# An encoder block on one core: the RWKV recurrence is given one plain tile layout, and its stages are emitted in small steps of several units in turn

## The chip, the core and the metric

The kernel runs on one core of one Trainium2 chip. Its time is the device time in microseconds of one execution, from the runs' own clock. Three runs of the kernel before took 3280.66, 3298.37 and 3299.71 us, so the median is 3298.37 us. A separate profiled execution took 3270.93 us.

## What is computed

The input is one sequence of 2048 tokens of width 1024, in float32. It is RMS-normed and projected into two groups of columns. Group A (1792 columns) is an RWKV-7 mixer of 8 heads of width 64, group B (1536 columns) is a differential attention of 4 heads. Their outputs go through one output projection and a residual, and then through a gated feed-forward block with a causal convolution of width 3.

The mixer is the part that the change touches. Its core is a scan over the tokens, one 64x64 state per head:

```python
def step(S, inp):
    r_t, w_t, k_t, v_t, a_t, b_t = inp
    sa = jnp.einsum('bhvk,bhk->bhv', S, a_t)
    S = (S * w_t[:, :, None, :] + sa[..., None] * b_t[:, :, None, :]
         + v_t[..., None] * k_t[:, :, None, :])
    return S, jnp.einsum('bhvk,bhk->bhv', S, r_t)
...
y = _rwkv7_scan(r_h, w_h, k_h, v_h, -kk, kk * a_h)
mean = jnp.mean(y, axis=-1, keepdims=True)
...
return (y * g.astype(jnp.float32)).astype(h.dtype)
```

The attention needs the projections of all three of its inputs, and the output projection needs both groups for a block of tokens.

## The kernel before

The kernel is written with tile pools and a scheduler. The program text gives each instruction a place, `high_priority(offset)` moves its priority that many instructions forward, and the scheduler then fixes one order per engine. Each engine works its own order off in sequence, so an instruction whose input is late holds up all that stand behind it.

**Phase 1** has two kinds of work. The first is projections. For each of four blocks of 512 tokens (`tb`), `proj_rwkv` makes the 14 column blocks of group A (tile `mm`, 128x512, lines L211 to L213: every product is made of three, from a high and a low half of each operand). `shift` writes them to scratch in memory. Afterwards `token_major` makes the columns of group B for the blocks in the order 3, 0, 1, 2 (tile `mm`, 128x256, L243 to L245), and `finish_qk` normalizes, transposes and stores the queries and keys.

The second kind is the recurrence, `rwkv(u)`, for 16 units of 128 tokens. A unit has two chunks of 64 tokens, four pairs of heads (`i`), and two heads in a pair (`hd`). With all heads side by side it does this:

- First part: norms and decays (`st`, `lpw`, `lpa`, `nb`, `sb`), then the products inside a chunk (`sa`, L448, K = 64 rows), masked by DVE into three tiles (L450 to L452), and transposes `bt`.
- Inverse: a triangular matrix per head and chunk is sent through memory (`ed`, `el`) into another layout, solved by 31 pairs of small DVE instructions (L482, L483), and sent back (`wd`, `tt`). Two small products `zp` (L520, L527, 32x32) complete it.
- Chain, one chunk after the other, because the state of one is the input of the next: `gp` (L543), `up` (L551), `hu` (L559), and the output `y`, to which two products are added in turn for each head, L569 with 128 rows and L571 with 64 rows.
- Outputs: the normalization of `y`, the gate product (L586) and a store to `yd`.

`after` is called once per two projected column blocks and emits one unit's first part and inverse, and the rest of the unit before the last two (`LAG = 2`), all with a priority offset of 3000. Where a float32 product is not in the split form above, one matmul of the program is two records in the trace.

**Attention** (`heads`) may start when the last unit is done, because it takes over the recurrence's pools. Nine of its steps are placed between the projections of group B, one per column block (`HEADS1 = 9`, offset 400). One head for a block of 256 queries takes scores `sc` (L725, L726), a DVE pass with mask and maximum (L729), exponentials on ACT, transposes `at`, products `po` with the values and a transpose `ott` (L813). **Feed-forward** for the first 512 tokens starts with `mixed` and `out_proj` (tile `up`, L905 to L907), which need the eight heads of the first two query blocks; its large products are L966 to L968 and L1009 to L1011.

Of the kernel before, what the change touches and what calls it, by code (L numbers as in the profile page):

```python
# [19 lines left out]
P = 128  # L20
# [8 lines left out]
XUB = 7  # L29
SUB, LRB, PUB, UB = 3, 3, 3, 2  # L30
# [9 lines left out]
LAG = 2  # L40
# [99 lines left out]
def phase1(g, ctx):  # L140
# [38 lines left out]

    def spread(tb):  # L180

        rs = rsa[:, 4 * tb:4 * tb + 4]
        rx = dn.tile([P, 4, P], F32, name="rx", tag="x", bufs=XB)
        nc.vector.tensor_copy(rx, rs.unsqueeze(2).broadcast_to((P, 4, P)))
        ps = ps_mm.tile([P, 4, P], F32, name="tp", tag="mm")
# [46 lines left out]
    def token_major(tb, hT, gi):  # L232
# [4 lines left out]
        for jj in range(2):  # L237
            for q in range(KT // 2):
                for j2 in range(2):
# [6 lines left out]
                    if q == KT // 2 - 1:  # L246
                        yield 2 * jj + j2, ps

    def proj_qk(tb, hT, gi):
# [12 lines left out]
        return lambda: finish_qk(tb, gi, qz, rs)  # L262

    def finish_qk(tb, gi, qz, rs):
# [3 lines left out]
        for hl_ in range(2):  # L268
# [15 lines left out]

    def proj_v(tb, hT, gi):
# [5 lines left out]

    w = load_w("w_in_a", 12, 4, P, True)
# [3 lines left out]
    stats(0)  # L296
    rb = spread(0)
# [9 lines left out]
    mask = cp.tile([P, P], F32, name="mask")  # L307
    nc.sync.dma_start(out=mask, in_=a["c_mask"])
# [42 lines left out]
    for i in range(UB):  # L351
        tts.append(cp.tile([P, NCH, GP, C], F32, name=f"tt{i}"))
        nc.gpsimd.memset(tts[i], 0.0)
# [4 lines left out]
    hc = cp.tile([P, GP, C], F32, name="hc")  # L358
    nc.vector.memset(hc, 0.0)
    def rwkv(u):  # L360
# [8 lines left out]
        r = sp.tile([P, GP, SB], F32, name="zl", tag="zl", bufs=1)  # L369
# [3 lines left out]
        xm = [sp.tile([P, GP, 2, P], F32, name="xm", tag="xm", bufs=XUB) for c in range(NCH)]  # L373
        bk = [sp.tile([P, GP, P], F32, name="bk", tag="bk", bufs=XUB) for c in range(NCH)]
        rb = sp.tile([P, GP, 2, C], F32, name="rb", tag="rb", bufs=(XUB + 1) // 2)
        lr = sp.tile([P, NCH, GP, C], F32, name="lr", tag="lr", bufs=LRB)
# [3 lines left out]
        for p in range(GP):  # L380
            nc.scalar.activation(sq[:, p], k[:, p], AF.Square, scale=v("kk", p))
        st = ps_tp.tile([P, GP, 2], F32, name="st", tag="tp")
        for p in range(GP):
            nc.tensor.matmul(st[:, p, :], sq[:, p], ones2, start=True, stop=True)
        nst = 2 * GP
# [4 lines left out]

        lpw = ps_tp.tile([P, GP, SB], F32, name="lpw", tag="tp")
        for p in range(GP):
            nc.tensor.matmul(lpw[:, p], wda[0:64, p * P:(p + 1) * P], zw[0:64], start=True, stop=True)
        thw = sp.tile([P, GP, SB], F32, name="thw", tag="thw")
        for p in range(GP):
            nc.scalar.activation(thw[:, p], lpw[:, p], AF.Tanh, bias=hw0[:, p:p + 1], scale=0.5)
        lpa = ps_tp.tile([P, GP, SB], F32, name="lpa", tag="tp")
        for p in range(GP):
            nc.tensor.matmul(lpa[:, p], wda[64:128, p * P:(p + 1) * P], zw[64:128], start=True, stop=True)
        kh = sp.tile([P, GP, SB], F32, name="kh", tag="kh")  # L400
        for p in range(GP):
            nc.scalar.activation(kh[:, p], lpa[:, p], AF.Tanh, bias=hw0[:, 4 + p:5 + p], scale=0.5)
# [18 lines left out]
        for c in range(NCH):  # L421
            cs, kc, uc = slice(c * C, c * C + C), slice(c * C, c * C + C), slice(C - c * C, 2 * C - c * C)
            for hd in range(2):
                q = hb[hd]
                nc.vector.tensor_mul(xm[c][q, :, hd, 0:C], kkn[q, :, cs], pp[q, :, c, 0:C])
                if hd == 0:
                    nc.vector.tensor_mul(bk[c][:, :, uc], kkn[:, :, cs], an[:, :, cs])
                nc.vector.tensor_mul(xm[c][q, :, hd, C:2 * C], r[q, :, cs], pp[q, :, c, 1:C + 1])
            nc.vector.tensor_mul(bk[c][:, :, kc], kh[:, :, cs], pin[:, :, cs])
# [4 lines left out]
        nc.gpsimd.tensor_mul(rkh, kh, r)  # L434
        sb = ps_tp.tile([P, GP, 2], F32, name="sb", tag="tp")
# [5 lines left out]
        def mk(q, a, b):  # L441
            return mask[q, a:b].unsqueeze(1).broadcast_to((64, GP, b - a))
# [11 lines left out]
        bkt = bk  # L454
        for c in range(NCH):
            ps = ps_sc.tile([P, GP, P], F32, name="bt", tag="sa")
            bs = bk[c]
# [680 lines left out]
```

## Time and profile before

| | value |
|---|---|
| median of three runs | 3298.37 us |
| profiled execution | 3270.93 us, its span 3269.2 us |
| TensorE (PE) busy | 3136.8 us, 96% of the span |
| VectorE (DVE) busy | 2085.0 us, 64% |
| ScalarE (ACT) busy | 1524.9 us, 47% |
| GpSimd (POOL) busy | 661.0 us, 20% |
| mean granted clock of PE | 0.972 |

Busy time of PE counts each matmul from its start to the end of its result, and matmuls overlap in the pipeline. A busy PE is therefore not one that issues as fast as it can: how fast it issues is read from the distance between the starts of neighbouring rows.

### The profile page before, as it was taken

How to read it: one execution, taken by the hardware profiler on the slowest of the kernel's cores; microseconds unless marked ns; L12 is line 12 of the kernel's file. 1: busy time of each engine (PE TensorE's matmuls, PEld its weight loads, DVE VectorE, ACT ScalarE, POOL GpSimd, SP SyncE). 2: the span in 40 equal slices, each digit the busy share in tenths (PEclk: the TensorE clock that was granted, in tenths of full speed). 3: DMA queues.
4: the chain of work that ended last, by engine and by line, in shares of the span. 5: the costliest groups of instructions: out<-in, count | busy, mean ns of one | idle time of the engine just before them, and what ended most of it. 6: DMA issues, size and time to landing. Idle time of an engine off the chain costs nothing.

```text
span 3269.2 us, 54217 instructions
## 1 busy us (share of the span) xinstructions
PE 3136.8 (96%) x19314; PEld 2657.6 (81%) x19314; DVE 2085.0 (64%) x5939; ACT 1524.9 (47%) x3391; POOL 661.0 (20%) x501
## 2 busy tenths in 40 slices
PE   8999999999999898899999999999998999999999
PEld 6777777888888788788878888888888888888887
DVE  4788778888873565667777786666533444444444
ACT  5666555655645564444445565444423322222221
POOL 4112113342322013254444111111100000000000
PEclk9989999989999899999999999999999999999999
DMA  9765544345464977556556756565574132223222
GB/s 298 252 210 155 189 141 152 105 134 153 126 183 132 290 233 262 160 192 204 197 196 222 234 174 203 168 206 184 192 281 153 65 116 84 97 91 107 87 97 97
DMA packets 395006, 557.43 MB, mean 171 GB/s; under 512 B 82544, under 2 KB 209776, under 8 KB 394608
## 3 DMA queue, kind: packets, MB, share of 16 engines
q1 hardware_dynamic: 394736, 553.97, 52.9%
q8 instruction: 153, 2.51, 0.3%
q14 instruction: 117, 0.96, 0.1%
HBM read 440.59 MB, written 113.25 MB: 169 GB/s over the span
## 4 chain that ended last, share of the span: by engine, by line
PE 80%; DMA 9%; DVE 8%; ACT 1%; issue 1%; SPq 1%; POOL 0%; DVEq 0%; ACTq 0%; POOLq 0%
PE up L968 9%; PE up L966 9%; PE up L967 9%; PE dn L1010 5%; PE dn L1009 5%; PE dn L1011 5%; PE mm L213 3%; PE mm L211 3%; PE mm L212 3%; PE mm L243 2%; PE y L571 2%; PE y L569 2%; PE mm L244 2%; PE mm L245 2%; PE up L906 2%; DMA fwlo<-lo_w_out 2%
## 5 line engine op out<-in xcount | busy, mean ns | idle before, releaser
L967 PE MATMUL up<-hT,fwhi 128*128 128x512 f32 (+1 forms) x1536 | 581.3, 379 | 0.0
L966 PE MATMUL up<-hT,fwhi 128*128 128x512 f32 (+1 forms) x1536 | 575.4, 378 | 3.7 <-DVE halo L975 2.8
L968 PE MATMUL up<-hT,fwlo 128*128 128x512 f32 (+1 forms) x1536 | 571.6, 378 | 7.0 <-DMA fwlo<-lo_w_ffn_up 7.0
L973 DVE SCALAR_TENSOR_TENSOR yy<-up,vec,yy 128x511 f32<-128x511 f32 x352 | 262.0, 744 | 346.2 <-ACT yy L970 345.9
L1012 DVE TENSOR_TENSOR acc<-dn,acc 128x512 f32<-128x512 f32 x352 | 237.0, 688 | 184.0 <-PE dn L1011 183.2
L968 PEld LDWEIGHTS up<-hT,fwlo 128*128 128x128 f32 x1536 | 292.2, 190 | 62.6 <-DMA fwlo<-lo_w_ffn_up 10.4
L966 PEld LDWEIGHTS up<-hT,fwhi 128*128 128x128 f32 x1536 | 290.2, 190 | 57.8 <-issue 4.3
L967 PEld LDWEIGHTS up<-hT,fwhi 128*128 128x128 f32 x1536 | 291.9, 190 | 52.4
L996 POOL TENSOR_TENSOR gl<-yy,gh 128x512 fp32r<-128x512 f32 (+1 forms) x64 | 106.0, 1656 | 1006.4 <-ACT gh L995 821.8
L117 ACT CAST fwhi<-fwraw 128x1024 fp32r<-128x1024 f32 x164 | 172.5, 1052 | 266.1 <-PE up L967 185.5
L970 ACT ACTIVATE yy<-up,vec 128x512 f32<-128x512 f32 x176 | 136.6, 777 | 301.2 <-PE up L968 295.9
L1010 PE MATMUL dn<-dlo,gh 128*128 128x512 f32 x704 | 276.1, 393 | 0.9 <-DMA dlo<-lo_w_ffn_down 0.9
L729 DVE CUSTOM_DVE_ANT_0 e<-sc,nd 128x512 f32<-128x512 f32 (+3 forms) x320 | 188.3, 607 | 136.9 <-PE sc L726 112.9
L1009 PE MATMUL dn<-dhi,gh 128*128 128x512 f32 x704 | 272.5, 396 | 0.5 <-ACT gh L995 0.5
L1011 PE MATMUL dn<-dhi,gl 128*128 128x512 f32 x704 | 261.9, 393 | 0.1
L243 PE MATMUL mm<-whi,hh 128*128 128x256 f32 x768 | 232.7, 304 | 11.9 <-DVE qlo L105 5.4
L244 PE MATMUL mm<-wlo,hh 128*128 128x256 f32 x768 | 227.2, 297 | 7.7 <-DMA wlo<-lo_w_in_b 7.5
L245 PE MATMUL mm<-whi,hl 128*128 128x256 f32 x768 | 225.0, 296 | 0.0
L736 ACT ACTIVATE e<-e,nm 128x1024 f32<-128x1024 f32 (+4 forms) x192 | 171.9, 898 | 53.3 <-DVE nm L733 52.9
L211 PE MATMUL mm<-hh,whi 128*128 128x512 f32 x448 | 187.8, 421 | 9.2 <-ACT hh L201 6.9
L117 ACT CAST whi<-wraw 128x512 fp32r<-128x512 f32 x208 | 127.8, 619 | 138.5 <-PE mm L212 61.8
L213 PE MATMUL mm<-hh,wlo 128*128 128x512 f32 x448 | 187.2, 419 | 2.1 <-POOL wlo L119 2.1
(278 smaller groups left out, 7322.6 us busy)
## 6 DMA issues: line engine op xcount, KB each, us to landing
fwraw<-in_w_ffn_up_dram SPq DMA_DIRECT2D x132, 512.0 KB, 5.5
fwlo<-lo_w_ffn_up SPq DMA_DIRECT2D x88, 512.0 KB, 5.0
draw<-in_w_ffn_down_dram SPq DMA_DIRECT2D x132, 256.0 KB, 4.3
vg<-vd SPq DMA_DIRECT2D x128, 256.0 KB, 4.3
wraw<-in_w_in_a_dram SPq DMA_DIRECT2D x112, 256.0 KB, 3.5
wraw<-in_w_in_b_dram SPq DMA_DIRECT2D x96, 256.0 KB, 5.1
lo_w_ffn_up<-fwlo SPq DMA_DIRECT2D x44, 512.0 KB, 2.9
dlo<-lo_w_ffn_down SPq DMA_DIRECT2D x88, 256.0 KB, 4.9
```

The source lines that it names most:

```text
L117: nc.scalar.copy(hi, raw)
L211: nc.tensor.matmul(ps, whi[k], hh[k], start=k == 0, stop=False)
L213: nc.tensor.matmul(ps, wlo[k], hh[k], start=False, stop=k == KT - 1)
L243: nc.tensor.matmul(ps, hh[k][:, ts_], whi[k], start=k == 0, stop=False)
L244: nc.tensor.matmul(ps, hh[k][:, ts_], wlo[k], start=False, stop=False)
L245: nc.tensor.matmul(ps, hl[k][:, ts_], whi[k], start=False, stop=k == KT - 1)
L966: nc.tensor.matmul(ps[:, q], wh[:, k % 4, cs], xh, start=k == 0, stop=False)
L967: nc.tensor.matmul(ps[:, q], wh[:, k % 4, cs], xl, start=False, stop=False)
L968: nc.tensor.matmul(ps[:, q], wl[:, k % 4, cs], xh, start=False, stop=k == KT - 1)
L1009: nc.tensor.matmul(ps, gh_[:, tsl], dh_, start=gi == 0, stop=False)
L1010: nc.tensor.matmul(ps, gh_[:, tsl], dl_, start=False, stop=False)
L1011: nc.tensor.matmul(ps, gl_[:, tsl], dh_, start=False, stop=gi == FG - 1)
```

## The change

- The recurrence gets one layout. `xm`, `lr`, `rb` and `sh` go. `ar` holds both left operands and `bk` both right ones, for both chunks, and `sm` holds the whole masked product. Twelve DVE instructions that build operands become four wide ones, and twelve masking instructions per unit become four of 128x512.
- The state lives in two fixed tiles `hs`, one per chunk.
- In the chain, one product `gy` (128 rows, 128 columns) makes what `gp` and L569 made apart. Two groups of eight further products are added to it, one before `up` and one after `hu`, each group in one piece.
- Pairs of products on the lower and the upper 64 rows (`sa`, `lpw` and `lpa`), or on two groups of 32 rows (`zp`), stand next to each other in the program.
- `rwkv(u)` yields 22 times. `tick` takes one step each of the oldest unit in the chain, of one in its outputs, of one in its inverse, and one or two steps of a unit's first part; `after` makes seven ticks (`STEPS`), and at most three units are under way between first part and chain (`UNITS`).
- The transposes of `finish_qk` are put off into the next column block's products, and `spread` into the next token block's first product.

```diff
-LAG = 2
+STEPS = 7
+UNITS = 3
...
@@ token_major
                     if q == KT // 2 - 1:
                         yield 2 * jj + j2, ps
+                if 4 * jj + q in (4, 6) and fins:
+                    fins.pop(0)()
...
+    stage = {n: [] for n in ("first", "ahead", "inverse", "ready", "chain", "last")}
+    def step(n, to):
+        with tc.high_priority(offset=HP):
+            if stage[n] and next(stage[n][0], "next") == "next":
+                unit = stage[n].pop(0)
+                if to:
+                    stage[to].append(unit)
+    def tick():
+        nonlocal ticks
+        ticks += 1
+        st = stage
+        if not st["chain"] and st["ready"]:
+            st["chain"].append(st["ready"].pop(0))
+        behind = len(st["ahead"]) + len(st["inverse"]) + len(st["ready"])
+        if not st["inverse"] and not st["ready"] and (len(st["ahead"]) > 1 or st["ahead"] and not st["first"] and (not units or behind + len(st["chain"]) == UNITS)):
+            st["inverse"].append(st["ahead"].pop(0))
+        behind = len(st["ahead"]) + len(st["inverse"]) + len(st["ready"]) + len(st["chain"])
+        if not st["first"] and units and (units[0] + 1) * SB <= done * TB and behind < UNITS:
+            st["first"].append(rwkv(units.pop(0)))
+        step("chain", "last")
+        step("last", None)
+        step("inverse", "ready")
+        for _ in range(1 + (ticks % 2 or not st["chain"])):
+            step("first", "ahead")
...
@@ rwkv, first part
-            for hd, q, q_ in ((0, lo_, hi_), (1, hi_, lo_)):
-                sa = ps_sc.tile([P, GP, P], F32, name="sa", tag="sa")
-                for i in range(GP):
-                    nc.tensor.matmul(sa[:, i, :], bk[c][q, i, :], xm[c][q, i, hd, :], start=True, stop=True)
-                kb, ub = hb[c], hb[1 - c]
-                nc.vector.tensor_mul(lr[q, c], sa[ub, :, 0:C], mk(ub, 0, C))
-                nc.vector.tensor_mul(rb[ub, :, hd], sa[ub, :, C:], mk(ub, C, P))
-                nc.vector.tensor_mul(xm[c][q_, :, hd], sa[kb], mk(kb, 0, P))
+            sa = [ps_sc.tile([P, GP, P], F32, name="sa", tag="sa") for hd in range(2)]
+            for i in range(GP):
+                for hd, q in enumerate(hb):
+                    nc.tensor.matmul(sa[hd][:, i, :], bk[q, i, c], ar[q, i, c], start=True, stop=True)
+            for hd in range(2):
+                nc.vector.tensor_mul(sm[c][:, :, hd], sa[hd], mk[c])
+            yield
...
@@ rwkv, chain (before: gp, up, hu as below, one head after the other)
-            for hd in range(2):
-                for i in range(GP):
-                    nc.tensor.matmul(y4[yq, i, hd, :], xm[c][:, i, hd, C:2 * C], sh[c][:, i, hd, :],
-                                     start=True, stop=False)
-                    nc.tensor.matmul(y4[yq, i, hd, :], rb[ub, i, hd, :], su[c][ub, i, hd, :],
-                                     start=False, stop=True)
+            gy = ps_y.tile([P, GP, 2, C], F32, name="gy", tag="y")
+            for i in range(GP):
+                nc.tensor.matmul(gy[:, i], ar[:, i, c], h[:, i], start=i == 0, stop=False)
+            for n, (i, hd) in enumerate(ih):
+                nc.tensor.matmul(gy[ub, i, hd], sm[c][kb, i, hd, ub], su[c][kb, i, hd], start=False, stop=n == len(ih) - 1)
+            gt = sp.tile([P, GP, 2, C], F32, name="gt", tag="gt")
+            nc.scalar.copy(gt[ub], gy[ub])
+            yield
+            up = ps_ch.tile([P, GP, 2, C], F32, name="up", tag="ch")
+            for i, hd in ih:
+                nc.tensor.matmul(up[ub, i, hd], tt[ub, i, hd], gt[ub, i, hd], start=True, stop=True)
+            nc.scalar.copy(su[c][ub], up[ub])
+            yield
+            hu = ps_ch.tile([P, GP, C], F32, name="hu", tag="ch")
+            for i in range(GP):
+                for hd, q in enumerate(hb):
+                    nc.tensor.matmul(hu[q, i], bk[:, i, c, q], su[c][:, i, hd], start=True, stop=True)
+            for hd, q in enumerate(hb):
+                nc.vector.tensor_add(h_[q, :, hd], hu[q], hp[q])
+            for n, (i, hd) in enumerate(ih):
+                nc.tensor.matmul(gy[kb, i, hd], sm[c][:, i, hd, kb], su[c][:, i, hd], start=False, stop=n == len(ih) - 1)
+            nc.scalar.copy(yt[kb], gy[kb].rearrange("p i h d -> p (i h d)"))
+            yield "next" if c == NCH - 1 else None
...
@@ phase 1
-            after(tb)
+            after()
+        done = tb + 1
```

Three places show how the order moves on PE. The first is the end of a chunk of the chain. Before, the two products for `y` (L569 and L571) alternate, and `hu` stands among them:

```order
L571 MATMUL y<-su,rb 64x64
L569 MATMUL y<-sh,xm 64x64
L571 MATMUL y<-su,rb 64x64
L559 MATMUL hu<-su,bk 64x64 x8
L569 MATMUL y<-sh,xm 64x64
L571 MATMUL y<-su,rb 64x64
```

In the change, a chunk's products stand in blocks of one shape, here with projections (`mm`) between two of them:

```order
L577 MATMUL gy<-hs_481,ar 128x128 x4
L579 MATMUL gy<-su,sm 64x64 x8
L246 MATMUL mm<-whi,hl_13619 128x256
...
L585 MATMUL up<-gt,tt_471 64x64 x8
L278 MATMUL tp<-ident,qz 128x128 x3
...
L591 MATMUL hu<-su,bk 64x64 x8
L595 MATMUL gy<-su,sm 64x64 x8
```

The eight alternations per head half are gone from the end of the chunk.

The second place is the products `sa` of a chunk. The numbers tell the two tiles `sa` apart, which belong to the lower and the upper 64 rows. In the change they stand in turn, with another unit's or stage's instruction between some of them:

```order
L490 MATMUL sa_1254<-ar_1161,bk_1162 128x128
L490 MATMUL sa_1255<-ar_1161,bk_1162 128x128
L490 MATMUL sa_1254<-ar_1161,bk_1162 128x128
L481 MATMUL sb_1247<-rk2_446,rkh_1245 128x2 x4
L490 MATMUL sa_1255<-ar_1161,bk_1162 128x128
L490 MATMUL sa_1254<-ar_1161,bk_1162 128x128
L490 MATMUL sa_1255<-ar_1161,bk_1162 128x128
```

Before, four of one stand together, then four of the other.

The third place is between two of the first attention heads (`ott` ends one, `sc` begins a later one). Before, the projections of group B fill the room between them:

```order
L813 MATMUL ott<-ident,ot 128x128 x2
L272 MATMUL tp<-ident,qz 128x128 x4
L725 MATMUL sc<-kg,qs 128x512
L726 MATMUL sc<-kg,qs 128x512
L725 MATMUL sc<-kg,qs 128x256
L726 MATMUL sc<-kg,qs 128x256
L243 MATMUL mm<-whi,hh_14131 128x256
L244 MATMUL mm<-wlo,hh_14131 128x256
L245 MATMUL mm<-whi,hl_14139 128x256
```

In the change the heads stand almost alone:

```order
L832 MATMUL ott<-ident,ot 128x128 x2
L796 MATMUL at<-ident,e_13287 128x128
L796 MATMUL at<-ident,e_13314 128x128 x2
L820 MATMUL po<-ah,vg 128x256
L823 MATMUL po<-ah,vg 128x128
L824 MATMUL po<-al,vg 128x128
L825 MATMUL po<-ah,vg 128x128
L826 MATMUL po<-al,vg 128x256
L827 MATMUL po<-ah,vg 128x256
L924 MATMUL up<-fwhi,yT_15079 128x256
L832 MATMUL ott<-ident,ot 128x128 x2
```

Before, 864 products `mm` of 128x256 stand behind the last one for `y`, and in the change 215 stand behind the last `gy`.

## Rows read from the trace of the kernel before

**Rows 1.** The page's first part: busy time, share of the span, instructions.
```profile
PE 3136.8 (96%) x19314; PEld 2657.6 (81%) x19314; DVE 2085.0 (64%) x5939; ACT 1524.9 (47%) x3391; POOL 661.0 (20%) x501
```
**Rows 2.** Stages: length, busy time of five engines, granted clock, DMA share, GB/s.
```profile
240.00:1075.00 835.00, 808.46 (x6882) 681.93 (x6880) 640.32 (x2099) 475.54 (x1402) 227.85 (x214) 0.94 0.50 150
1075.00:1228.00 153.00, 133.14 (x937) 123.53 (x938) 94.97 (x449) 97.93 (x330) 18.18 (x13) 0.91 0.83 254
1228.00:1249.00 21.00, 13.31 (x85) 10.33 (x84) 16.58 (x49) 13.07 (x25) 1.46 (x1) 1.00 0.85 303
1249.00:1321.00 72.00, 65.84 (x501) 62.62 (x501) 38.19 (x114) 28.70 (x50) 29.57 (x14) 0.97 0.81 254
1321.00:3269.00 1948.00, 1895.28 (x9801) 1602.70 (x9800) 1130.57 (x2724) 761.15 (x1220) 327.99 (x200) 0.99 0.48 158
```
**Rows 3.** Waits of PE: total us, times, longest.
```profile
PE mm L243 <- DVE qlo L105: 5.4, 2, 4.6
PE tp L187 <- DVE rx L184: 3.2, 2, 2.5
```
**Rows 4.** Timeline of PE: blocks of one shape, and what follows each.
```profile
609.37 0.97 PE L543 MATMUL gp<-sh,xm 128*64 128x64 f32 x16
610.27 0.38 PE L437 MATMUL sb<-rk,rkh 128*128 128x2 f32 x2
...
615.45 1.05 PE L384 MATMUL st<-ones,ksq 128*128 128x2 f32 x8
616.36 0.36 PE L245 MATMUL mm<-whi,hl 128*128 128x256 f32 x1
```
**Rows 5.** Timeline of PE, outputs of a chunk: start, length, instruction.
```profile
600.20 0.33 PE L569 MATMUL y<-sh,xm 128*64 128x64 f32 x2
600.46 0.33 PE L571 MATMUL y<-su,rb 64*64 64x64 f32 x2
...
602.51 0.32 PE L571 MATMUL y<-su,rb 64*64 64x64 f32 x2
```
**Rows 6.** Timeline of PE: a change of shape from `mm` to `zp` and back.
```profile
607.55 0.28 PE L245 MATMUL mm<-whi,hl 128*128 128x256 f32 x1
607.67 0.28 PE L243 MATMUL mm<-whi,hh 128*128 128x256 f32 x1
...
607.88 0.69 PE L520 MATMUL zp<-t,lr 32*32 32x32 f32 x16
608.49 0.39 PE L243 MATMUL mm<-whi,hh 128*128 128x256 f32 x1
```
**Rows 7.** Timeline of PE: `sa` alone, and `sa` beside `lpw`.
```profile
611.88 1.16 PE L448 MATMUL sa<-xm,bk 64*128 64x128 f32 x8
612.96 0.39 PE L245 MATMUL mm<-whi,hl 128*128 128x256 f32 x1
...
621.24 0.27 PE L393 MATMUL lpw<-zw,wda 64*128 64x128 f32 x1
621.25 0.27 PE L448 MATMUL sa<-xm,bk 64*128 64x128 f32 x1
621.36 0.27 PE L393 MATMUL lpw<-zw,wda 64*128 64x128 f32 x1
621.36 0.27 PE L448 MATMUL sa<-xm,bk 64*128 64x128 f32 x1
```
**Rows 8.** Timeline of DVE: first unit's last mask, first transpose behind its solve.
```profile
128.38 0.69 DVE L452 TENSOR_TENSOR xm<-sa,mask 64x512 f32<-64x512 f32 x1
...
175.96 0.43 DVE L494 STREAM_TRANSPOSE t<-tt 32x256 f32<-32x256 f32 x1 [2.93 <-DMA tt<-wd]
```
**Rows 9.** By line: durations ns min/median/max, first and last start us.
```profile
L813 PE MATMUL ott<-ident,ot x64: 270/272/476, 1084.9 to 2355.5; 128*128 128x128 f32 x64
```
**Rows 10.** Timeline of PE: the eighth head's last product.
```profile
1213.82 0.38 PE L813 MATMUL ott<-ident,ot 128*128 128x128 f32 x2
```

More of the change, by code (lines that the diff above doesn't have):

```diff
@@ L357, in phase1 @@
         nc.gpsimd.memset(eye[q * 32:q * 32 + 32].rearrange("l j t -> l (j t)")[:, q::36], 1.0)
-    hc = cp.tile([P, GP, C], F32, name="hc")
-    nc.vector.memset(hc, 0.0)
+    hs = []
+    for c in range(NCH):
+        hs.append(cp.tile([P, GP, 2, C], F32, name=f"hs{c}"))
+        nc.vector.memset(hs[c], 0.0)
     def rwkv(u):
@@ L384, in rwkv @@
             nc.tensor.matmul(st[:, p, :], sq[:, p], ones2, start=True, stop=True)
+        yield
+        lpw = ps_tp.tile([P, GP, SB], F32, name="lpw", tag="tp")
+        lpa = ps_sc.tile([P, GP, SB], F32, name="lpa", tag="sa")
+        for p in range(GP):
+            for l, q in ((lpw, lo_), (lpa, hi_)):
+                nc.tensor.matmul(l[:, p], wda[q, p * P:(p + 1) * P], zw[q], start=True, stop=True)
+        thw = sp.tile([P, GP, SB], F32, name="thw", tag="thw")
+        kh = sp.tile([P, GP, SB], F32, name="kh", tag="kh")
+        for l, t, b in ((lpa, kh, 4), (lpw, thw, 0)):
+            for p in range(GP):
+                nc.scalar.activation(t[:, p], l[:, p], AF.Tanh, bias=hw0[:, b + p:b + p + 1], scale=0.5)
+        yield
         nst = 2 * GP
@@ L535, in rwkv @@
+        for b in range(2):
+            nc.scalar.copy(zt[r2[b]], zp[r2[b], 0])
+        yield
+        for i, hd in ih:
+            for b in range(2):
+                nc.tensor.matmul(zp[r1[b], 1, i, hd], zt[r2[b], i, hd], tt[r2[b], i, hd, 32:64], start=True, stop=True)
+        for b in range(2):
+            nc.scalar.copy(tt[r1[b], :, :, 32:64], zp[r1[b], 1])
+        yield "next"
+        w = GP * P
+        yt = sp.tile([P, w], F32, name="yt", tag="yt", bufs=2)
         for c in range(NCH):
+            kb, ub, h, h_ = hb[c], hb[1 - c], hs[c], hs[1 - c]
@@ L593, in rwkv @@
         nc.gpsimd.tensor_add(yt, yt, vt)
+        yield
+        yield
+        yield
+        y = ps_sc.tile([P, w], F32, name="y", tag="sa")
+        nc.tensor.matmul(y, zg, wgu, start=True, stop=True)
         nc.vector.tensor_mul(yt, y, yt)
         nc.sync.dma_start(out=g.yd[u * SB:(u + 1) * SB, :], in_=yt)
-    units = list(range(g.ntb * TB // SB))
-    started = []
-    def unit():
-        if units:
-            with tc.high_priority(offset=HP):
-                started.append(rwkv(units.pop(0)))
-                next(started[-1])
-        if started and (len(started) > LAG or not units):
-            with tc.high_priority(offset=HP):
-                next(started.pop(0), None)
     def head():
@@ L611, in head, with after, rest @@
             next(g.heads, None)
-    def after(done):
-        if (units and (units[0] + 1) * SB <= done * TB) or (started and not units):
-            unit()
-        if not units and not started and g.att is None and 2 in g.phases:
+    def after():
+        for _ in range(STEPS):
+            tick()
+        rest()
+    def rest():
+        if not units and not any(stage.values()) and g.att is None and 2 in g.phases:
             rctx.close()
@@ L648, in phase1 @@
                 nh += 1
-    while units or started:
-        after(nb)
+    while units or any(stage.values()):
+        tick()
+    after()
     if 2 not in g.phases:
```

194 lines of the change are left out of this document (70 added, 124 removed).

## The prediction

> **What bounds the kernel now.** I read the page's busy times first, then the table by stages, then PE's timeline inside phase 1, the waits of PE, and last the order of the changed program. PE is busy for 96% of the span [rows 1], so a gain must come from PE issuing less, issuing faster, or standing still less. The stages [rows 2] say where: the recurrence runs with the projections from about 240 to 1075 us, attention starts at 1075 while projections of group B are still being made, these end at 1228, and from 1321 on it is feed-forward with attention, 1948 us that the change does not touch. All that can change lies in the first 1321 us. There DVE is busy for 640 of 835 us in the recurrence and for 95 of 153 in the first attention stretch, so it is a second candidate, but not the one that ends most waits: PE's named waits are few [rows 3]. The recurrence therefore costs what its products cost on PE, and what counts is the distance between starts.
>
> These distances differ greatly for like work. In a block of one shape, 16 records `gp` take from 609.37 to 610.27 us, 0.056 us each, and 8 of `st` take 0.91 us, 0.114 each [rows 4]. For `y`, where records with 128 and with 64 rows alternate in twos, nine such steps go from 600.20 to 602.51 us: 0.257 for two records, 0.128 each, though they have the 64 columns of `gp` [rows 5]. A change of shape costs time at the edges of blocks too: `mm` follows `mm` after 0.12 us, but `zp` follows it after 0.21 [rows 6]. So one change of shape costs about 0.09 us. The third thing to see is two kinds of product on the two halves of the rows: 8 `sa` alone take 1.08 us (0.135 with their edges, and 0.112 by the step within a kind), but `sa` beside `lpw` start within 0.01 us of each other and the next pair comes 0.11 us later [rows 7]. Both run at once.
>
> **The change part by part**, on PE's time, against the profiled execution of 3270.93 us (27 us under the median of the runs, 3298.37).
>
> *Outputs of a chunk.* Before: 8 heads times two products times two records are 32 records at 0.128, 4.1 us, and `gp` 0.90, together 5.0. After: four products `gy` with 128 columns (8 records at 0.114, 0.91 us), eight with 64 rows (16 at 0.056, 0.90) and eight more at the end (0.90), together 2.7. Saved: 2.3 us for each of 32 chunks, **-73 us**. `up` and `hu` keep their number. Bounds: if adding to the same result is the cost and not the change of shape, 32 records keep 0.05 us each, which leaves -22; if the larger `gy` issues as fast as `gp`, -88.
>
> *Pairs of `sa`.* 256 products are 512 records at 0.112. In the new order only 105 of the 224 possible neighbours inside a chunk really stand side by side (the second place in the order shows why); each such pair hides one record: 105 x 0.112 = **-12 us**. Bounds 0 and -25. `lpw` and `lpa` stand in separate blocks of four in the new order: 0.
>
> *Pairs of `zp`.* Of 512 products 407 have a neighbour on the other group of rows. At 0.036 us per record (16 in 0.61 us, with edges [rows 6]) full overlap as in [rows 7] would give up to -15. In [rows 7] the two results were different tiles; here both go to one tile `zp`. The Trainium skill ("TensorEngine Tiling (Array Packing)", Gotcha 1: PSUM Pressure) says that different row tiles cannot access the same PSUM bank simultaneously. By that rule this term is 0, by the pairs of the trace it is -15; no row here shows such a pair on one tile. I take 0, because the step of 0.036 us is already small.
>
> *More changes of shape elsewhere.* Because steps of several units are emitted in turn, the order mixes their products more. Outside `y` I count 465 changes of shape up to the start of attention before, and 669 in all in the new order (there `gy` is included). 204 x 0.09 = **+18 us**; +10 to +30.
>
> *DVE and ACT.* Twelve operand products per unit become four, twelve masks become four. That is work off the bounding engine, so I cost it at nothing; PE covers it. It gives room to the solve, below.
>
> *Waits that go.* The transposes of the queries no longer stand right behind their own normalization (the 5.4 us of L243 behind `qlo`), nor `spread` in front of the first product (3.2 us) [rows 3]: **-7 us**, 0 to -9. Next in line there is only the next `mm`.
>
> *Where the recurrence ends.* The first part of a unit is now held back until there is room (three units), and the inverse until the next unit is ahead. In the order, 215 `mm` are left behind the last product of the chain, against 864 before; behind the first scores 77 are left, against 665. So 588 x 0.12 = 71 us of projections leave the stretch of the first heads and fill the recurrence instead. They are not lost, but the heads lose their cover. From the end of the first head to that of the eighth it took 1213.8 - 1084.9 = 129 us [rows 9, 10]. Without 71 us of projections PE would need 58. DVE's load there is 95/153 of 129, 80 us [rows 2], but this holds the splitting of queries, keys and values, which goes with the projections. Where the projections had just ended (1228 to 1249) DVE was busy for 16.6 of 21 us, 79%. At that share 50 to 80 us of DVE work take 63 to 101 us, 5 to 43 more than PE needs. I take **+15**, near the lower end because the projections' share goes.
>
> *The solve.* A unit's first `zp` waits for its way through memory, 31 steps on DVE and back. The first unit took 47.6 us from its last mask to the first transpose behind the solve (128.38 to 175.96) [rows 8]. Priced with the steps above, PE has 57 to 131 us of other work between a unit's last `sa` and its first `zp` in the old order, and 35 to 123 in the new one; the least are 35, 41 and 46. Against 47.6 this lacks 13 + 7 + 2, and the granted clock of 0.94 stretches it a little: **+8**, 0 to +22.
>
> *Clock.* The mean of 0.94 in the recurrence [rows 2] means some 12% of 835 us at 1.2 GHz. Fewer slow stretches like `y` may raise it, the heads without cover may lower it: **-8**, between -20 and +10.
>
> Sum: -73 - 12 + 0 + 18 - 7 + 15 + 8 - 8 = **-59 us**. The profiled execution becomes 3212, and the median 3239 us, 1.8% less.
>
> **The rivals.**
>
> *The heads keep their pace.* Then seven heads again take 129 us, now with only 58 us of PE work in them: +71 instead of +15, the sum is -3, and the median 3295. For it: scores, maximum, exponential, transposes and values follow one another over three engines, and DVE was busy for only 62% of the filled stretch. Against it: just behind the projections DVE was at 79% [rows 2], and there the heads' products alternated with projections by priority, so their own chain did not set the pace.
>
> *The solve ends last (slower).* If the way through the solve takes 65 us instead of 47.6, because the wide masks and the state updates of two other units stand between its 62 small instructions in DVE's order, PE stands still at `zp` in nine of the 16 units. The shortfall against the new order's room, stretched by 6% for the clock, is 130 us. The sum is -59 - 8 + 130 = +63, and the median 3361. It outweighs the gain from about 57 us on. Against it: DVE has some 16 instructions per unit less, and DVE was well occupied when the first unit took 47.6. For it: everything behind `zp` on PE, projections included, waits with it.
>
> *The alternation is not what costs.* If records that add to an earlier result are slow as such, the outputs give -22 and not -73, and the sum is -8: 3290, no change.
>
> **How the numbers follow.** The forecast gets a chance of 0.62, the heads' pace 0.17, the solve 0.14, the alternation 0.07. The predicted time is the forecast's, 3239 us. Its own bounds reach from about 3185 (full pairs and a better clock) to 3270. The range must also take in the two rivals without change, up to 3300 with the scatter of the runs, and leaves out the solve: 3185 to 3302. A difference under 1%, 33 us, can't be told from no change in this kernel. Of the forecast nine tenths lie beyond it, which with the halves of the rivals gives 0.60 for faster; no change holds the heads' pace, most of the alternation and the rest, 0.26; slower is the solve, 0.14.
>
> **What would show it.** In the changed profile `gy` with 64 columns should step at about 0.056 us per record in blocks; if it steps at 0.11 or more, the first term is wrong. `sa` records should start in twos. PE's waits should show `zp` or the products with `t11` behind DVE or the transfer of `tt` with under 25 us in all; over 60 means the solve. The first scores should start near 1075 us again, and the first large feed-forward product (1321 before) should come near 1260. If attention starts on time and that product comes after 1300, the heads kept their pace. If attention itself starts later than 1110, the recurrence is what was priced wrongly.

## The result and the profile after

The changed kernel takes 3301.14 us (median of 20 runs, 3292.53 to 3314.14), the kernel before 3277.59 us (20 runs); the ratio is 1.0065, 95% interval 1.0049 to 1.0081. Forecast were 3239 us and a gain of 59 us; the change costs 24 us. The 20 runs put the kernel before 21 us under the median of three, 3298.37, that the forecast started from. The profiled executions, before and after, have spans of 3269.2 and 3294.6 us.

The stages of the changed kernel, cut where the kernel before was cut in [rows 2]: length, busy time of five engines, granted clock, DMA share, GB/s.

```profile
240.00:1153.00 913.00, 857.58 (x7148) 749.20 (x7146) 605.99 (x2000) 520.67 (x1534) 233.77 (x214) 0.90 0.54 161
1153.00:1180.00 27.00, 21.81 (x127) 18.90 (x127) 17.67 (x98) 12.37 (x38) 1.29 (x1) 0.75 0.88 272
1180.00:1208.00 28.00, 17.46 (x88) 13.67 (x86) 18.57 (x107) 16.12 (x50) 1.27 (x1) 0.82 0.81 259
1208.00:1332.00 124.00, 106.17 (x705) 94.82 (x704) 88.03 (x332) 63.66 (x127) 40.06 (x22) 0.90 0.73 224
1332.00:3294.00 1962.00, 1899.67 (x9788) 1603.36 (x9786) 1122.11 (x2722) 758.81 (x1218) 327.91 (x200) 0.99 0.48 157
```

Attention starts at 1153 instead of 1075, and the clock in the recurrence is 0.90 instead of 0.94. The first eight heads then need little time: from the end of the first to that of the eighth it takes 1236.5 - 1166.0 = 70 us, against 129 before [rows 9, 10].

```profile
L832 PE MATMUL ott<-ident,ot x64: 270/272/476, 1166.0 to 2362.9; 128*128 128x128 f32 x64
1236.53 0.44 PE L832 MATMUL ott<-ident,ot 128*128 128x128 f32 x2
```

The first large feed-forward product comes at 1332 instead of 1321, and the untouched rest takes 1962 instead of 1948 us.

The products themselves, in PE's timeline (start, length, instruction): first `zp`, which answers to [rows 6], then the outputs of a chunk, which answer to [rows 5].

```profile
565.41 0.69 PE L557 MATMUL zp<-t,sm 32*32 32x32 f32 x32
566.04 0.39 PE L244 MATMUL mm<-whi,hh 128*128 128x256 f32 x1
...
713.98 1.05 PE L577 MATMUL gy<-hs,ar 128*128 128x128 f32 x8
714.97 1.14 PE L579 MATMUL gy<-su,sm 64*64 64x64 f32 x16
716.04 1.16 PE L435 MATMUL lpa<-zw,wda 64*128 64x128 f32 x8
...
723.78 0.69 PE L591 MATMUL hu<-su,bk 128*64 128x64 f32 x16
724.29 1.10 PE L595 MATMUL gy<-su,sm 128*64 128x64 f32 x16
725.32 0.39 PE L244 MATMUL mm<-whi,hh 128*128 128x256 f32 x1
```

The outputs of this chunk take 0.99 + 1.07 + 1.03 = 3.1 us against 5.0 before. Over all 32 chunks, by the mean distance behind their records at full clock, a chunk takes 3.43 us against 4.99. 32 records of `zp` take the 0.69 us that 16 took in [rows 6], and 16 of `hu` 0.51 us: both kinds run two at once. But elsewhere the steps of several units cut one another up. A little earlier in the same timeline:

```profile
572.36 0.37 PE L563 MATMUL zp<-tt,zt 32*32 32x32 f32 x10
572.66 0.33 PE L591 MATMUL hu<-su,bk 128*64 128x64 f32 x2
572.92 0.24 PE L563 MATMUL zp<-tt,zt 32*32 32x32 f32 x2
573.09 0.33 PE L591 MATMUL hu<-su,bk 128*64 128x64 f32 x2
...
574.02 0.33 PE L595 MATMUL gy<-su,sm 128*64 128x64 f32 x2
574.28 0.24 PE L563 MATMUL zp<-tt,zt 32*32 32x32 f32 x2
574.45 0.33 PE L595 MATMUL gy<-su,sm 128*64 128x64 f32 x2
```

Two records of each in turn, 0.43 us for four: this is the alternation that the change had taken out of `y`. And the waits of PE from 240 to 1396 us (in total, times, longest; [rows 3] of before had 5.4 behind `qlo`):

```profile
PE sc L744 <- DMA qs<-qd: 9.5, 6, 3.2
PE mm L244 <- ACT qz L258: 9.3, 7, 2.8
PE mm L244 <- DVE qlo L106: 6.5, 3, 4.3
PE mm L245 <- DMA wlo<-lo_w_in_b: 6.2, 4, 3.6
PE mm L244 <- ACT hh L202: 5.9, 6, 3.2
```

**One account for all kernels.** I took the distances between the starts of all PE records up to the 614th of the 6144 `up` records of the feed-forward (output projection included), and split what exceeds the price of each record at full clock: distances over 0.6 us are "standing", the longer price at half clock (1.2 instead of 2.4 GHz) is "clock", and the rest, less what runs at once, is "issue" (changes of shape and slow series). "Reach" is the time of that product, "rest" from there to the last PE start. The experiments e1 to e18 follow in the next section. The same program up to there differs by 7 to 10 us between two executions (before and e6, changed and e5, e1 and e7), so smaller differences say nothing. The work up to that mark is almost the same: e1 and e7 have done 57 records more there than the kernel before, e9, e10, e15 and e16 68 more, some 9 us, which their "rest" then lacks. Each row is one profiled execution; those of e3, e7, e9 and e13 lie 6 to 11 us above the median of their kernel's runs, those of e10, e15 and e17 8 to 10 below.

| kernel | reach | issue | standing | clock | rest |
|---|---|---|---|---|---|
| before / e6 | 1389 / 1399 | 163 / 163 | 88 / 88 | 65 / 75 | 1876 / 1876 |
| changed / e5 | 1396 / 1403 | 114 / 113 | 120 / 125 | 90 / 93 | 1894 / 1882 |
| y grouped, e1 / e7 | 1390 / 1400 | 99 / 98 | 121 / 130 | 91 / 92 | 1886 / 1866 |
| half solve: before e9, grouped e10, changed e8 | 1413, 1349, 1410 | 160, 101, 115 | 93, 110, 131 | 79, 58, 90 | 1861, 1863, 1869 |
| no low weights: before e13, grouped e11, changed e12 | 1406, 1331, 1405 | 164, 94, 117 | 71, 106, 132 | 92, 58, 85 | 1876, 1880, 1883 |
| pairs alone e18, with y e15, and sa e16 | 1394, 1370, 1359 | 134, 76, 70 | 101, 115, 121 | 82, 97, 88 | 1867, 1856, 1851 |

Change less kernel before: issue -49, standing +32, clock +26, rest +18. With e5 less e6 it is -50, +37, +18 and +6, so clock and rest are the uncertain two.

### The profile page after: what moved, and what is told of

The parts are those of the page before. It is cut to its first block, busy times and chain, and to the rows that moved or that the text cites. A ratio compares the mean times of both kernels' runs of the same rounds, so it can differ in the third digit from the quotient of the medians.

```text
span 3294.6 us, 53252 instructions
## 1 busy us (share of the span) xinstructions
PE 3125.0 (95%) x19058; PEld 2654.8 (81%) x19058; DVE 1994.2 (61%) x5668; ACT 1515.7 (46%) x3311; POOL 662.5 (20%) x501
## 4 chain that ended last, share of the span: by engine, by line
PE 72%; DVE 11%; DMA 10%; ACT 3%; issue 2%; SPq 2%; POOL 0%; ACTq 0%; DVEq 0%; POOLq 0%
PE up L987 9%; PE up L985 9%; PE up L986 9%; PE dn L1029 5%; PE dn L1030 4%; PE dn L1028 4%; PE mm L214 2%; PE mm L212 2%; DMA fwlo<-lo_w_ffn_up 2%; PE mm L213 2%; PE mm L244 2%; PE up L925 2%; PE mm L246 2%; PE mm L245 2%; PE up L926 2%; PE sa L490 2%
## 5 line engine op out<-in xcount | busy, mean ns | idle before, releaser
L992 DVE SCALAR_TENSOR_TENSOR yy<-up,vec,yy 128x511 f32<-128x511 f32 (+1 forms) x352 | 261.7, 743 | 378.4 <-ACT yy L989 378.3
L213 PE MATMUL mm<-hl,whi 128*128 128x512 f32 x448 | 185.3, 414 | 0.1
```

The lines of the kernel that those rows point to most:

```text
L213: nc.tensor.matmul(ps, whi[k], hl[k], start=False, stop=False)
L992: nc.vector.scalar_tensor_tensor(yn[:, d:], ps[:, 0:512 - d], w, yn[:, d:], ALU.mult, ALU.add)
```

## The experiments

**Does y's alternation cost what its steps show?** e1 is the kernel before with

```
-  for hd: for i: y <- xm, sh (start=True); y <- rb, su
+  all eight y <- xm, sh (start on the first only); then all eight y <- rb, su
```

> The kernel before with one edit: in a chunk the eight products of y with 128 rows stand together, and behind them the eight with 64 rows, instead of one of each per head. Nothing else of the change is in it. If the alternation of shapes is what costs (first term of the prediction), 32 records at 0.128 us become 32 at about 0.056 plus two changes of shape, 2.1 us less for each of 32 chunks: about -65 us, ratio 0.98, and the attention's first scores come some 65 us sooner. Rival: records that add to an earlier result are slow as such, or PE had that time to spare while it waited for the next operands: between -22 and 0 us, ratio 0.993 to 1.0.

Measured: 3284.28 us, ratio 1.0020 (1.0009 to 1.0032). The steps fell nearly as forecast: in e1's timeline 16 records take 1.1 us, and 14 of the second kind 1.0; `gp` and `y` of a chunk take 3.07 us against 4.99 in the mean. The view by line (durations, first and last start) has the first scores at 1006.8, 68 us sooner than in [rows 2].

```profile
401.27 1.15 PE L569 MATMUL y<-sh,xm 128*64 128x64 f32 x16
404.16 1.02 PE L572 MATMUL y<-su,rb 64*64 64x64 f32 x14
```
```profile
L726 PE MATMUL sc<-kg,qs x320: 220/393/793, 1006.8 to 2259.1; 128*128 128x512 f32 x136, 128*128 128x128 f32 x8, 128*128 128x256 f32 x8, 128*128 128x384 f32 x8
```

So the first term's mechanism is right, but none of it arrives. The early scores are in part a matter of order: from 240 us to them PE starts 6545 records, in [rows 2] 6882, and the other 337 follow behind. Waits of e1 from 240 to 1390 us, then two of the kernel before in the same stretch, then the stages of e1:

```profile
PE mm L244 <- DMA wlo<-lo_w_in_b: 15.2, 6, 4.2
PE sa L448 <- DVE wl L483: 13.8, 3, 5.5
PE sc L726 <- DMA qs<-qd: 10.2, 5, 3.6
```
```profile
PE mm L244 <- DMA wlo<-lo_w_in_b: 7.5, 8, 3.6
PE sc L725 <- DMA qs<-qd: 2.8, 4, 1.2
```
```profile
240.00:1007.00 767.00, 721.26 (x6545) 625.22 (x6545) 625.32 (x2056) 448.10 (x1310) 222.36 (x211) 0.91 0.51 151
1007.00:1226.00 219.00, 186.51 (x1313) 176.01 (x1314) 122.49 (x532) 128.03 (x439) 25.57 (x17) 0.89 0.78 237
```

DVE is busy for 82% of the recurrence (77% in [rows 2]), `sa` waits behind the last instruction of the solve (`wl`), weights and queries come later than before, and the clock falls from 0.94 to 0.91.

**The order of the feed-forward.** Only `HA`, which sets the heads of that stage ahead, is changed in e5 (changed kernel) and e6 (before): `-HA = 0` `+HA = 20`; e7 is e1 with `+HA = 1`.

> The changed kernel with one number changed that only acts behind the recurrence: the attention heads of the feed-forward stage are put 20 places ahead (HA 20, not 0). By the order the heads of the second feed-forward block then end behind 1200, 1322, 1483, 1624, 1771 and 1910 of its products, where the changed kernel has 1182, 1268, 1439, 1583, 1704 and 1870 and the kernel before 1190, 1346, 1486, 1622, 1769 and 1911; the order up to the first feed-forward product is that of the change. Theory that part of the loss is not in the recurrence at all but in this order, which the change moved without touching its code: the traces show 501 us for the work between the 30% and 50% marks of these products plus 70% in the kernel before and 522 in the changed one, so about -18 us, 3283. Rival: the order there is indifferent and the 20 us are scatter of one profile: 3301 plus or minus 5.

> The kernel before with the same one number (HA 20), so that its feed-forward order is the same as that of the changed kernel with HA 20 but for one head; the order of its first stage is its own. Both theories: within 5 us of the kernel before, since its order there was already the good one. Against the changed kernel with HA 20 it shows what the change is worth without the feed-forward order: by the traces up to the first tenth of the feed-forward products (1389 us before, 1396 after) the changed one is still 5 to 8 us slower; if the change's own gain was only hidden by the order, it is 20 us or more faster.

> The kernel before with y grouped, and HA 1: its feed-forward order then has the second block of the kernel before (1190, 1346, 1486, 1622, 1769, 1911), where grouped y alone had fallen into the other one (1166, 1248, 1406, 1562, 1700, 1850). Theory of the order: about -18 us against grouped y alone, 3266, ratio to before 0.997. Rival (the order is indifferent): 3284. Both say that of the 63 us of issue time that grouping takes out of the recurrence at most some 10 reach the end.

Measured: e5 3292.01, ratio 1.0031 (1.0012 to 1.0050); e6 3276.04, 1.0001 (0.9979 to 1.0022); e7 3261.11, 0.9938 (0.9918 to 0.9958). e1 and then e7 in one stretch of the feed-forward:

```profile
1900.00:2140.00 240.00, 225.67 (x1240) 191.67 (x1238) 166.41 (x473) 123.88 (x217) 26.02 (x19) 0.97 0.59 184
```
```profile
1900.00:2140.00 240.00, 230.90 (x1305) 198.12 (x1304) 171.22 (x475) 125.98 (x220) 26.96 (x21) 0.99 0.58 186
```

The same 240 us hold 1240 records in one order and 1305 in the other. One number that only acts behind the recurrence is worth 9 us to the changed kernel and 23 to e1. In these traces the order of that stage differs between kernels that differ only ahead of it, so part of a ratio here can be that order. At nearly equal order the change still costs 10 to 16 us (by the ratio, or by e5 against e6).

**Who takes the saving?** Less VectorE: `-for s in range(31)` `+for s in range(0, 31, 2)` in the changed kernel (e8), before (e9), y grouped (e10). Fewer transfers: the low weights not fetched again, in y grouped (e11), changed (e12), before (e13); both in the changed one (e17). These kernels no longer compute the function: they leave out half of the solve, or take the high half of a weight for the low one.

> The changed kernel with HA 20, and 15 of the 31 steps of each unit's solve left out: 480 instructions of 0.28 us on VectorE, some 134 us of its work (what it computes there is then not the inverse). PE's work is the same. If PE's waits and the half clock in the recurrence come from VectorE's queue and the way through the solve, the time that PE was to gain appears: about -40 us against the changed kernel with HA 20, 3252. Rival: PE's own issue and its clock bound the stretch, VectorE only follows: 0 to -10 us, 3282 to 3292.

> The kernel before with HA 20 and the same 15 steps of the solve left out. PE's named waits behind VectorE in its recurrence are some 20 us. Theory that y's slow stretches give VectorE its time: the solve is hidden there, so only -5 to -15 us, 3261 to 3271. Rival: VectorE bounds the kernel before as well, -40 us or more.

> The kernel before with y grouped, HA 20 and the same 15 steps of the solve left out (its second feed-forward block is in the order of the kernel before). Its recurrence had 82% VectorE occupation and 17 us of PE's waits of sa behind the solve's last instruction. If VectorE takes back what grouping saves, then against the kernel before with half a solve grouping now gives 45 us or more instead of 16: 3261 - 45 = 3216 or less. Rival (the clock and the attention stretch take it back): 16 to 25 us, about 3240 to 3250.

> The kernel before with y grouped and HA 1, and in all projections but the first of each weight the low halves of the weights are not fetched (the high half stands in their place, so the projections are not exact): some 35 MB of transfers less up to 1240 us, PE's products the same in number and shape. With grouped y PE waited 15 us behind these fetches and 13 us behind those of the queries, with DMA busy for 78% of the attention stretch. If transfers take back what grouping saves: -25 us against grouped y with HA 1, 3236. Rival: these waits only show who is late, and others take their place: 3261 plus or minus 8.

> The changed kernel with HA 20, and the low halves of the projections' weights are not fetched but for the first use of each weight (the high half stands in their place, so the projections are not exact). Its PE waited 11 us behind these fetches and 12 behind those of the queries even with half a solve. If transfers limit its recurrence, as they did with grouped y alone: -40 us against the changed kernel with HA 20, 3252. Rival: its limit is the order of the products of group B and of their splits on ScalarE and VectorE: 0 to -12 us, 3280 to 3292.

> The kernel before with HA 20 and the same fetches left out. If its slow y gave the transfers time, they are hidden there: -5 to -15 us against 3276, 3261 to 3271, as half a solve gave it -3. Rival: transfers end last in the attention stretch of every version: -40 us, 3236.

> The changed kernel with HA 20, with both reliefs at once: 15 of the 31 solve steps left out, and the low halves of the projections' weights not fetched but for the first use of each (the projections are not exact). Each alone gave it nothing (-8 and +2 us). If the two limits stand behind each other in the changed order: -35 us or more against 3292, 3257 or less. Rival: neither is its limit; what holds it is PE's own issue (mixed shapes, 62 us of changes behind 200 us where grouped y alone has 44) and the half clock that goes with it: 3280 to 3296.

Measured, ratio to before: e8 3283.53, 1.0009 (0.9990 to 1.0029); e9 3273.52, 0.9978 (0.9949 to 1.0006); e10 3228.26, 0.9836 (0.9800 to 0.9872); e11 3219.99, 0.9819 (0.9784 to 0.9854); e12 3294.52, 1.0059 (1.0035 to 1.0082); e13 3277.91, 1.0007 (0.9991 to 1.0024); e17 3277.20, 0.9988 (0.9963 to 1.0014). The recurrence of e10 and of e11:

```profile
240.00:978.00 738.00, 704.66 (x6542) 613.41 (x6540) 535.83 (x1630) 447.97 (x1307) 221.46 (x210) 0.94 0.53 157
```
```profile
240.00:1004.00 764.00, 722.24 (x6692) 631.66 (x6690) 624.49 (x2070) 459.29 (x1381) 226.47 (x213) 0.93 0.43 126
```

This is the clearest finding. Either relief is worth at most 4 us to the kernel before (e9, e13); with either, grouping y is worth 45 us (e10 against e9) or 58 (e11 against e13) of the 64 us of issue that it saves in the account (163 - 99), and the clock is back at 0.94 and 0.93. The order of the feed-forward is no rival for the 45: behind the mark e9 and e10 have the same order and take 1861 and 1863 us. So y's slow series were cover for the solve and the transfers: PE was busy in them, but only with time that the others needed. In the changed kernel one relief gives 8 us (e8) or none (e12), both together 15 (e17), between the two expectations (35 or none), and its issue does not fall. Even these gains can't be put down to the recurrence: against e5, e8's reach is 7 us later and e17's 9 us earlier (1394), which is scatter, while their rest is 13 us shorter (1869 both), with another order of the feed-forward.

**The emission, the finish and the pairs of the change.** e2 emits one unit at a time, as before, with the new layout; e3 puts the finish of queries and keys behind the next column block again; e4 takes the pairs apart (`-for i: for hd` `+for hd: for i`); e14 is e3 with half a solve.

> The changed kernel with its layout, products and buffers, but its units emitted as before: the whole first part and inverse of one unit at a time, and the rest of the oldest at once, no steps of several units in turn. By the order it has 387 changes of shape up to the first scores against 716, but no projection is left beside the last unit's chain. If the mixing of steps is what cost the gain, 329 changes x 0.09 = 30 us go, and with them part of the 32 us of longer waits and 22 us of lost clock, against some 30 us for a last unit without cover: about 3260 us, ratio to before 0.995. Rival: the layout itself is slower than it was priced and the steps are what keeps it near the kernel before: 3330 us or more, ratio 1.016 or more.

> The changed kernel, but the four transposes and splits of queries and keys stand behind the next column block's products, as in the kernel before, not in the middle of them. The trace after shows 14 waits of the projections of group B behind ScalarE's reading of their own result tiles (qz and qlo), about 16 us, where the kernel before had 5.4. If the halves in the middle take a buffer from the projections, these waits go: about -12 us, 3289. Rival: the waits only show who was late and come back at the next product: 3301 plus or minus 6.

> The changed kernel, but products for the two halves of the rows or columns no longer stand side by side: sa, lpw and lpa, zp and hu run through one half first and the other behind it. If pairs run at once as the trace after suggests (hu at 0.029 us per record against 0.056 alone, 512 records twice; sa and zp some 20 us together), undoing them costs 30 to 50 us: about 3340, ratio to before 1.02. Rival: what pairs save is given back in the granted clock or in waits for VectorE: 3301 plus or minus 8.

> The changed kernel with queries and keys finished behind the next column block, as before (HA 0; by the order its second feed-forward block stands as in the kernel before), and with 15 of the 31 steps of the solve left out. Half a solve gave the changed kernel with HA 20 only -8 us. If the halves in the middle of the products keep that gain from showing: -30 us or more against 3276, 3246 or less. Rival: the way through the solve is no limit of the changed order at all: 0 to -10, 3266 to 3276.

Measured: e2 3411.24, ratio 1.0422 (1.0398 to 1.0446); e3 3276.24, 0.9996 (0.9982 to 1.0010); e4 3328.69, 1.0165 (1.0140 to 1.0190); e14 3294.61, 1.0035 (1.0014 to 1.0055). The recurrence of e2:

```profile
240.00:1262.00 1022.00, 846.88 (x7305) 756.32 (x7303) 619.57 (x1972) 524.60 (x1546) 244.14 (x222) 0.84 0.50 149
```

PE stands for 175 of 1022 us. Its longest waits there are for operands of a unit's own first part, 33.9 us of `sa` behind `bk` and 19.0 of `nb` behind `nx`, so with this layout the steps in turn are needed; why no other work stands between is not shown, and e2 cannot price the mixing. e3 gains 25 us, but its reach is 1410 (changed: 1396) and its rest 1868 (1894): the gain lies in the feed-forward, and that the halves in the middle cost waits is not shown. e4 confirms the pairs: undoing them costs 28 us against the changed kernel (33 by the ratios). e14 fits neither expectation: it is 18 us slower than e3 with less work; up to the first scores its trace has 746 changes of shape against 668, so the solve's share can't be read from it.

**Is any saving lost, or only y's?** `gp`, `up` and `hu` side by side (`-for hd: for i` `+for i: for hd`) in the kernel before (e18), with y grouped (e15); in e16 `sa` in pairs too, from two tiles.

> The kernel before with nothing but gp, up and hu in pairs of column halves, y still alternating, HA 0; its second feed-forward block has the order of the kernel before. 28 us less issue on PE, as with grouped y. Theory that y's slow stretches cover the work of the other engines and any other issue saved on PE arrives: -20 us, 3257. Rival: whatever PE saves in this recurrence is first taken by waits and clock: within 8 us of 3277; then the 21 us that pairs gave on top of grouped y came from the order around them.

> The kernel before with y grouped, HA 20, and gp, up and hu emitted so that the products of the two halves of the columns stand side by side, as hu does in the changed kernel (0.029 us per record there, 0.056 alone): 1024 records times 0.027 is 28 us less issue on PE, more if up pairs as well. Theory that PE's issue no longer sets the end once y is grouped: at most a third of it arrives, 0 to -10 us against 3261. Rival: 28 us or more arrive, 3233 or less, and the products' pairs are the part of the change worth keeping.

> The kernel before with y grouped, HA 20, gp, up and hu in pairs of column halves as in the run before this one (3240 us), and sa now also in pairs of row halves: 256 pairs of records at 0.112 us each, of which the second of a pair costs nothing where both run at once, 28 us less issue. If issue that is saved by pairs arrives as it did for gp, up and hu (21 of 28): 3220, ratio 0.983. Rival: the longer hold of two tiles by each pair and VectorE's masks behind them take it back: 3240 plus or minus 8.

Measured: e18 3269.55, ratio 0.9957 (0.9931 to 0.9982); e15 3240.26, 0.9892 (0.9861 to 0.9922); e16 3217.82, 0.9821 (0.9784 to 0.9858). e16, its recurrence and three of its blocks:

```profile
240.00:1022.00 782.00, 726.81 (x6720) 628.24 (x6718) 629.21 (x2069) 461.88 (x1387) 225.80 (x210) 0.89 0.52 154
```
```profile
509.94 1.16 PE L448 MATMUL sa<-xm,bk 64*128 64x128 f32 x16
511.70 0.68 PE L553 MATMUL up<-gt,tt 64*64 64x64 f32 x16
517.39 0.69 PE L561 MATMUL hu<-su,bk 128*64 128x64 f32 x16
```

16 records of `sa` take the 1.16 us that 8 took in [rows 7]. Alone the pairs bring 8 of their 28 us by the medians, behind grouped y 21 (e7 to e15); by the ratios it is 14 and 15, so the times don't settle whether they differ. The account suggests that they do: standing and clock rise with the first savings and are then at 209 to 222 us together in e1, e7, e15 and e16; why they stay there is not shown. e16 is 61 us faster than the kernel before and 83 faster than the change. By the account 30 to 40 us of the 61 lie ahead of the mark and 25 behind it, of which some 9 are work done earlier. It has like cheaper products without the change's steps: standing and clock as in the changed kernel (209 against 210), issue 70 against 114. Up to the first scores it has 37 blocks of at most four records of a shape other than 128x128, e1 39, the changed kernel 250, and reach differs by about those 44 us (1359 against 1396 to 1403). The other half of the 83, 43 us, lies behind the mark (1851 against 1894).

## Why the prediction was wrong

- **The bounding argument** failed: that PE is 96% busy [rows 1] and a gain "must come from PE issuing less". It holds, but a slow series counts as busy too, and less issue is not yet less time. The sum passed 67 us of saved issue on one to one and looked at DVE only as work that "PE covers". Grouped y shows it: 64 us of issue saved, and the result is 7 us worse (e1) or 16 better (e7), but 45 to 58 better once solve or transfers are relieved.
- **Outputs, -73:** mechanism right, size off. Forecast were 2.7 us per chunk; an undisturbed chunk takes 3.1, the mean of all is 3.43, so -50. The old emission with y grouped (e1, 3.07) has cheaper outputs than the change.
- **Pairs:** `sa` came as forecast: 143 of 420 distances between `sa` records are under 0.02 us, against 38 of 411 before, so 105 more, the number forecast. `zp` was put at 0 and is not (32 records in the time of 16); `hu` was overlooked: the change emits it in pairs of column halves (0.51 us for 16). Together the pairs are worth 28 us (e4), -12 was forecast.
- **More changes of shape, +18:** right in number (669 forecast, 671 in the trace) and in price: at full clock the record ahead of a change takes 0.10 us more than its own price in both kernels. All of PE's issue is -49 where -67 was forecast, and the outputs account for that.
- **Waits that go, -7:** the wait of `tp` for `rx` fell from 3.2 to 1.1 us, but the projections' waits behind the queries grew, from 5.4 behind `qlo` to 9.3 behind `qz` and 6.5 behind `qlo`. With the next two terms the sum put standing at +16; it grew by 32.
- **Heads, +15:** came as forecast, 70 us where 58 + 15 were expected; that rival falls.
- **Solve, +8:** its own working gives 22, or some 14 with the room stretched by 6%, not 8. In the trace PE waits 8.6 us at `zp` and, behind `tt`, at `up`, so the term came near by luck. The rival fell: its sign was over 60 us, and half a solve left the time nearly as it was (e8).
- **Clock, -8:** the largest error of a single term, +26, or +18 by e5 against e6. Half clock rose from 187 us (e6: 225) to 285 (e5: 308) by the clock's records. Grouped y alone has 287 and 273 (e1, e7), with a relief 186 and 192 (e10, e11), so the longer half clock comes with the limits that the reliefs lift there. In the changed kernel one relief leaves it at 271 and 269 (e8, e12).
- **The feed-forward, "which the change does not touch":** +18 in the profile, 9 by e5. Its order moved though its code didn't.

Of the 84 us between forecast and profile the account gives 34 to the clock, 18 to the feed-forward, 18 to issue and 16 to standing (two too many, since the work up to the mark is not quite the same). The sign that was named, attention later than 1110, came (1153), and with it what it stood for: the recurrence was priced wrongly. The range held the time only at its end, through the rivals without change, and by luck: its end of 3302 started from a median of 3298, and put on the 3277.59 us of 20 runs the same range ends at 3281.

Open: why neither relief alone helps the changed order, so that its standing and lost clock are measured but not explained; and what sends the clock down. In e13 standing fell by 17 us against e6 and the clock took 17 more, which hints that standing still is not its only reason; but this is one execution, 10 us above the median of its runs.

## What to carry to other kernels

An engine that is busy for 96% of the time may be busy slowly: before a saving on it is counted, halve the work of its suppliers, and see whether the saving appears only then. When a scheduler orders the program, compare the order of untouched stages too, and put it back before judging a change. Try cheaper products first without cutting their series up: like savings in the old emission gave 61 us where the new one lost 24, though about half of that difference lies in the feed-forward.

## What the runs showed of the hardware

- Products on the two halves of the columns run at once: 16 records of `hu` in 0.51 us, against 0.90 for 16 of `gp` [rows 4].
- Pairs of 32-row products ran at once though they write one tile (different partitions of it): 32 `zp` records in 0.63 us up to the next `mm`, 0.020 each, against 0.61 us for 16 in [rows 6]. The rule of the Trainium skill that was weighed ahead ("TensorEngine Tiling (Array Packing)", Gotcha 1: PSUM Pressure), that different row tiles can't access one bank simultaneously, would have given no gain; this case's trace does not bear it out.
- A change of shape cost the same in both kernels: up to the first scores, at full clock, the record ahead of it took 0.097 us more than its own price in the mean of 459 in the kernel before (without the steps of `y`), 0.100 in the mean of 569 in the changed one.
- Fewer waits did not bring clock in one execution: 240 to 1093 us of e13, with transfers relieved, ran at 0.89, against 0.94 in [rows 2].

```profile
240.00:1093.00 853.00, 836.59 (x6847) 705.41 (x6846) 627.97 (x2091) 470.17 (x1398) 223.47 (x212) 0.89 0.39 117
```
